# Two-block transformer on one core: modulations computed as dot products on VectorE, and tiles placed at multiples of 128 bytes

## The chip, the cores and the metric

One core of a Trainium2 chip runs the whole program. The metric is the device time of one execution in microseconds (us). About 0.5% is what a measurement of this kernel can tell from no change.

## What is computed

Batch 1, 512 latent tokens and 256 context tokens of 1024 channels, all in float32. The first block has two layers; each modulates its inputs by a condition vector `c` (latent) and `c_ctx` (context):

```python
for i in range(DEPTH):                      # 2 layers: windowed attention, then gated linear attention (GLA)
    m_lat = jnp.split((c_lat @ w_mod[i] + b_mod[i])[:, None, :], N_MOD, axis=-1)   # c_lat = silu(c)
    m_ctx = jnp.split(c_con @ w_mod[i] + b_mod[i], N_MOD, axis=-1)                 # c_con = silu(c_ctx)
    h_lat = modulate(x_lat, g_pre_mix[i], m_lat[0], m_lat[1])
    h_ctx = modulate(x_ctx, g_pre_mix[i], m_ctx[0], m_ctx[1])
    ...
def channel_mlp(h, w_in, w_out):
    return jnp.square(jax.nn.relu(h @ w_in)) @ w_out
```

`w_mod[i]` is 1024 x 6144, six modulations of 1024 numbers: m 0 and 1 shift and scale the mixer's input, 2 is the gate of its output, 3 to 5 the same for the MLP. A second block follows with a chunked attention, a state-space branch and a mixture of experts (MoE) of 16 experts, two per token.

## The kernel before, in words

Activations lie transposed in SBUF, channels on the partitions. A weight comes in units of 1 MB (128 x 2048 float32) by SP's queue into `raw`; `unit` (L209) splits it into two F32R tiles, `whi` by ScalarE (L213) and `wlo` by VectorE (L214), and every product is three F32R matmuls (`mm3`, `mm3s`, L229 to L244): high by high, high by low, low by high. In the first half of the MLP (`inproj`, L399) the weights are stationary and the activations `hl` (512 latent columns) and `hc` (256 context columns) move, in the second half (`natproj1`, L421, by `second`) the squared activations `hid` are stationary and 512 columns of the weights move. The MLP (L715) runs over 16 blocks of 256 hidden channels; in each it loads one unit of either matrix, does `first(b)` and `second([b - 1])`, squares on VectorE (L732, L733) and adds to `acc` on VectorE (L790). The order on each engine is the one in which the program is written, as a scheduler with priorities lays it out.

A modulation half (`mod_half`, L340) is 512 of the 1024 numbers of one m: two raw loads of 1 MB, 16 float32 matmuls with `csil` (silu of both condition vectors, padded to 32 columns) stationary and 256 weight columns moving (L354; 32 rows of the trace), a copy on ScalarE (L358), four transposes by `ident` on TensorE (L361), a sum and the bias on VectorE (L364, L366). 24 halves are computed: 4 in `first_norm`, 12 as filler between the score groups of `layer0_attn` (list `mods`, L562, L563), 8 between the heads of `layer1_mix` (L1076, L1115). The first MLP has no filler. `mod_affine` (L369) and `mod_gate` (L384) read what they give. In the GLA, `states` holds the recurrence over chunks (L1037, with S updated by VectorE at L1039), and L1055 to L1057 its outputs.

Constants are allocated first in one pool: `small` (vectors and biases), `ident`, `identb`, `mhalf`, then `csil`, `modT`, `aff`. Everything that comes after them, the pool of weight tiles first, begins where they end:

```python
self.c = e(tc.tile_pool(name="const", bufs=1))
self.w = e(tc.tile_pool(name="wstream", bufs=2))
```

Of the kernel before, what the change touches and what calls it, by code (L numbers as in the profile page):

```python
# [10 lines left out]
F32 = mybir.dt.float32  # L11
F32R = mybir.dt.float32r
BF = mybir.dt.bfloat16
I32 = mybir.dt.int32
U32 = mybir.dt.uint32
AF = mybir.ActivationFunctionType
ALU = mybir.AluOpType
AX = mybir.AxisListType
SP = mybir.EngineType.SP
P = 128  # L20
D = 1024
KC = 8
# [7 lines left out]
def _unit_in(w, c=256):  # L30
    k, n = w.shape
    return np.ascontiguousarray(
        w.reshape(k // P, P, n // c, c).transpose(2, 1, 0, 3).reshape(n // c, P, -1))


def _unit_out(w):
    k, n = w.shape
    return np.ascontiguousarray(
        w.reshape(k // 256, 2, P, n).transpose(0, 2, 1, 3).reshape(k // 256, P, -1))
# [37 lines left out]
def prep(i):  # L77
    o = {}
# [6 lines left out]
    cc[:, :, 1] = g("c_ctx").reshape(KC, P).T  # L85
    s.add("c", cc)
    for l in range(2):
        o[f"w_mod{l}"] = _unit_in(g("w_mod")[l])
        s.add(f"b_mod{l}", _cols(g("b_mod")[l]))
        for n in ("g_pre_mix", "g_post_mix", "g_pre_mlp", "g_post_mlp"):  # L90
            s.add(f"{n}{l}", _cols(g(n)[l]))
        o[f"w_mlp_in{l}"] = _unit_in(g("w_mlp_in")[l])
        o[f"w_mlp_out{l}"] = _unit_out(g("w_mlp_out")[l])
    o["w_qkv"] = _unit_in(g("attn_w_qkv")[0])
    perm = []
    for t in range(8):
# [51 lines left out]
class Kern:  # L148
    def __init__(self, tc, A, at):
        self.tc, self.nc, self.A, self.at = tc, tc.nc, A, at  # L150
        self.stack = ExitStack()
        e = self.stack.enter_context
        self.c = e(tc.tile_pool(name="const", bufs=1))
        self.w = e(tc.tile_pool(name="wstream", bufs=2))
        self.s = None
        self.t = e(tc.tile_pool(name="tiny", bufs=6))
        self.dram = e(tc.tile_pool(name="dram", bufs=1, space=bass.MemoryType.DRAM))
        self.p2 = e(tc.tile_pool(name="ps2", bufs=2, space=bass.MemoryType.PSUM))
        self.p1 = e(tc.tile_pool(name="ps1", bufs=4, space=bass.MemoryType.PSUM))
        nc = self.nc  # L160
        self.small = self.c.tile([P, A["small"].shape[1]], F32, name="small")
        nc.sync.dma_start(self.small, A["small"])
        self.ident = self.c.tile([P, P], F32, name="ident")
        make_identity(nc, self.ident)
        self.identb = self.c.tile([P, P], BF, name="identb")
        nc.vector.tensor_copy(self.identb, self.ident)
        self.n = 0
        self.norms = []
        self.sides = {"left": "left", "right": "right"}
        self.mhalf = self.c.tile([P, 4], F32, name="mhalf")  # L170
        nc.vector.memset(self.mhalf, -0.5)

    def right(self, name, bufs=1):
# [157 lines left out]

    def mod_init(self):
        nc = self.nc
        self.csil = self.c.tile([P, KC, 32], F32, name="csil")
        nc.vector.memset(self.csil, 0.0)
        nc.scalar.activation(self.csil[:, :, 0:2], self.sm("c").rearrange("p (k b) -> p k b", b=2), AF.Silu)
        self.modT = [self.c.tile([P, 48, 2], F32, name=f"modT{l}") for l in range(2)]
        self.aff = {}

    def mod_half(self, pool, l, m, half, tag="rows", raws=("raw", "raw"), own=None):  # L340
# [19 lines left out]
        for k in range(4):  # L360
# [5 lines left out]
        nc.vector.tensor_add(self.modT[l][:, c0:c0 + 4, :], self.modT[l][:, c0:c0 + 4, :],  # L366
                             bm[:, :, None].to_broadcast([P, 4, 2]))

    def mod_affine(self, l, which, ks=slice(0, KC)):  # L369

        nc = self.nc
        m0 = 0 if which == "mix" else 3
        if (l, which) not in self.aff:
            self.aff[l, which] = [self.c.tile([P, 2, KC], F32, name=self.nm("aff")) for _ in range(2)]
        sc, sh = self.aff[l, which]
        gp = self.sm(f"g_pre_{which}{l}")
        at = lambda m: slice(8 * m + ks.start, 8 * m + ks.stop)
        for b in range(2):
            nc.vector.scalar_tensor_tensor(sc[:, b, ks], self.modT[l][:, at(m0 + 1), b], 1.0, gp[:, ks],
                                           op0=ALU.add, op1=ALU.mult)  # L380
            nc.vector.tensor_copy(sh[:, b, ks], self.modT[l][:, at(m0), b])
        return sc, sh
# [96 lines left out]
def layer0_attn(K):  # L479
# [11 lines left out]
    with ExitStack() as left:  # L491
# [67 lines left out]
        op = K.opool.enter_context(K.right("oT"))  # L559
        oc = op.tile([P, KC, NCTX], F32, name="oTc")  # L560
        ol = op.tile([P, KC, L], F32, name="oTl")
        mods = [(0, m, x) for m in (2, 3, 4, 5) for x in range(2)]  # L562
        mods += [(1, m, x) for m in (1, 0) for x in range(2)]  # L563
        with K.right("att", 2) as ap:
            def scores(qb, j):

# [92 lines left out]
                pass  # L659
            w_o = [K.unit(A["w_o0"][u]) for u in range(2)]  # L660
            K.mod_affine(0, "mlp")
            K.mod_affine(1, "mix")
    return oc, ol, w_o


# [46 lines left out]
        finish(*last)  # L712


def mlp(K, l, hs, nts, finish, swap, side, split=False, filler=None):  # L715


    tc, nc, A = K.tc, K.nc, K.A
# [3 lines left out]
    with tc.tile_pool(name="mlp", bufs=1, side=side) as mp, tc.tile_pool(name="mlph", bufs=4, side=side) as hp:  # L722
# [74 lines left out]
        for b in range(1, NB):  # L797
            if b > 1:
                first(b)
            if b < NB - 1:  # L800
                second([b - 1])
            if filler and b == 1:

                z = hp.tile([P, nts[0] * P], F32, tag="hf0", name=K.nm("hf"), bufs=1)
                nc.vector.memset(z[:, 0:1], 0.0)
                K.anchor = z[:, 0:1]
            for _ in range(2 if filler else 0):
                next(filler, None)
        second([NB - 2, NB - 1])

# [1 line left out]
def layer0(K):  # L812
# [2 lines left out]
    oc, ol, w_o = layer0_attn(K)  # L815
    X = K.residual(K.ctx_pool)
    sc, sh = K.aff[0, "mlp"]
    sc1, sh1 = K.aff[1, "mix"]
    h = [None, None]
    hp, h_close = K.opened(K.left("h1l"))  # L820
    h[0] = K.pair(hp, "hl", [P, KC, L])
# [18 lines left out]
    with K.scratch(), K.right("gate") as gp:  # L840
        for i in (4, 5):
            pre(i, sc, sh, False)
        gates2 = []

        def swap():
            gates2.extend(K.mod_gate(0, "mlp", b, gp) for b in range(2))
            h_close.close()
            hp, K.h_close = K.opened(K.left("h2l"))
            hcp, K.hc_close = K.opened(K.left("h2c"))
            h[:] = [K.pair(hp, "hl", [P, KC, L]), K.pair(hcp, "hc", [P, KC, NCTX])]  # L850

        def finish2(i, y):
            K.postnorm(X[i], y, gates2[i // 4])
            pre(i, sc1, sh1, dv=2, pool=i < 4)
        mlp(K, 0, list(h), [4, 2], finish2, swap, "right")
    K.ctx_close.close()
    return X[:4], h

# [1 line left out]
def layer1_mix(K, hl, hc):  # L860
# [212 lines left out]
                nc.tensor.transpose(b[:, c * P:c * P + P], ys[c][:, t * P:t * P + P], K.ident)  # L1073
            a.copy(dst, b)

    mods = [(1, m, x) for m in (2, 4, 3, 5) for x in range(2)]  # L1076
    dec = {}
    tc.keep_in_program_order(a.preload_act_table_set("natural_log_exp_and_others"))
    u = K.unit(A["gla_in"][0])
# [24 lines left out]
    for h in range(6):  # L1104
        if h < 4:
            S[h] = states(h, dec[h])
        if h == 0:

            zero = K.tiny(1)
            v.tensor_scalar(zero, dec[3][1][2][:, 0, 0:1], 0.0, None, op0=ALU.mult)  # L1110
            for t in range(4):
                a.activation(og[:, t, :], og[:, t, :], AF.Silu, bias=zero)
                o = og[:, t, :].rearrange("p (h x) -> p h x", h=4)
                v.tensor_mul(o, o, gn[:, None, :].to_broadcast([P, 4, 256]))
        for i in range((2, 2, 1, 1, 1, 1)[h]):  # L1115
            K.mod_half(hp, *mods.pop(0), tag="ktc", raws=(("whi", "wlo"), ("raw", "raw"))[i])
        if 1 <= h < 5:
            Y[h - 1] = output(h - 1, *S[h - 1])
        if h >= 2:
            turn(*Y[h - 2])  # L1120
# [970 lines left out]
```

## Time and profile before

| what | us |
|---|---|
| median of 3 runs (2306.82 to 2314.99) | 2307.37 |
| the profiled execution | 2317.49 |
| its span | 2315.5 |
| TensorE busy (PE) | 2189.1 |
| VectorE busy (DVE) | 1307.3 |
| ScalarE busy (ACT) | 968.4 |
| GpSimd busy (POOL) | 284.2 |

Engine names in rows: PE is TensorE's matmuls, PEld its weight loads beside them, DVE VectorE, ACT ScalarE, POOL GpSimd, SP the engine that issues most DMAs. PEclk is the granted clock of TensorE, 1.00 its full 2.4 GHz. Matmuls overlap in the pipeline: one lasts longer in a row than the next one's start is behind its own, so that the distance of two starts tells what one costs. L12 is line 12 of the kernel. "a<-b" is a result and what it is computed from, with the number of the tile left out; of a matmul the operand that moves stands first.

### The profile page before, as it was taken

The page shows a single profiled execution, that of the slowest core. Times are in us where ns is not written, and L with a number is a line of the kernel's source. Part 1 is how long each engine was busy: PE and PEld are TensorE (multiplying, and loading weights), DVE is VectorE, ACT ScalarE, POOL GpSimd, SP SyncE. Part 2 cuts the span into 40 slices and gives each one's busy share as a digit, 9 for nine tenths or more (in the row PEclk, how much of TensorE's full clock was granted, in tenths as well). Part 3 has the DMA queues.
Part 4 walks back from the last instruction along what each step waited for, and adds up shares of the span by engine and source line. Part 5 has one row for each costly group of instructions (what it writes and reads, how often), then busy time and mean ns, then how long its engine had stood idle before and what let it go on. Part 6 is the DMA issues. An engine that isn't in the chain of part 4 may idle for free. (4 is left out here: it accounts for less than half of the span.)

```text
span 2315.5 us, 31205 instructions
## 1 busy us (share of the span) xinstructions
PE 2189.1 (95%) x12608; PEld 1795.7 (78%) x12608; DVE 1307.3 (56%) x2203; ACT 968.4 (42%) x1515; POOL 284.2 (12%) x301
## 2 busy tenths in 40 slices
PE   7999989999999999899999999999989997897996
PEld 5876658888888888789967887888789875686775
DVE  4666664435454444631864578555645854447885
ACT  5445555521121222542544543232354453435874
POOL 0024432000000000500000100000130000012321
PEclk9999999999999999999999999999999998998998
DMA  7223341211221121202353133422332335568993
GB/s 285 73 92 128 128 168 51 73 55 55 73 73 55 55 73 55 71 37 70 115 197 130 51 109 112 143 96 91 111 104 91 135 128 112 140 247 292 314 306 106
DMA packets 53746, 278.10 MB, mean 120 GB/s; under 512 B 8864, under 2 KB 13360, under 8 KB 25184
## 3 DMA queue, kind: packets, MB, share of 16 engines
q1 hardware_dynamic: 42080, 248.75, 30.7%
q0 software_dynamic: 10704, 25.68, 3.8%
q8 instruction: 100, 1.64, 0.3%
q10 hardware_dynamic: 816, 1.66, 0.2%
q14 instruction: 46, 0.38, 0.0%
HBM read 263.49 MB, written 24.08 MB: 124 GB/s over the span
## 5 line engine op out<-in xcount | busy, mean ns | idle before, releaser
L213 ACT CAST whi<-raw 128x2048 fp32r<-128x2048 f32 x106 | 202.4, 1910 | 551.2 <-PE b L244 381.6
L214 DVE TENSOR_TENSOR wlo<-raw,whi 128x2048 fp32r<-128x2048 f32 x106 | 245.2, 2315 | 270.8 <-ACT whi L213 264.9
L242 PE MATMUL b<-hl,whi 128*128 128x512 f32 (+1 forms) x736 | 284.0, 386 | 2.4 <-DVE t L315 1.8
L790 DVE TENSOR_TENSOR acc<-acc,b 128x512 f32<-128x512 f32 x280 | 179.9, 681 | 187.5 <-PE b L244 187.3
L240 PE MATMUL b<-hl,whi 128*128 128x512 f32 (+1 forms) x736 | 282.9, 385 | 0.8 <-ACT whi L213 0.8
L244 PE MATMUL b<-hl,wlo 128*128 128x512 f32 (+1 forms) x736 | 281.8, 386 | 0.0
L242 PE MATMUL b<-wlo,hid 128*128 128x512 f32 x640 | 216.1, 394 | 0.0
L240 PE MATMUL b<-whi,hid 128*128 128x512 f32 x640 | 214.8, 395 | 0.7 <-DVE acc L790 0.7
L244 PE MATMUL b<-whi,hid 128*128 128x512 f32 x640 | 214.0, 395 | 0.0
L242 PEld LDWEIGHTS b<-hl,whi 128*128 128x128 f32 x736 | 139.2, 189 | 30.3 <-issue 2.9
L240 PEld LDWEIGHTS b<-hl,whi 128*128 128x128 f32 x736 | 138.9, 189 | 30.2 <-ACT whi L213 1.3
L244 PEld LDWEIGHTS b<-hl,wlo 128*128 128x128 f32 x736 | 139.3, 189 | 28.2 <-issue 0.2
L1947 DVE TENSOR_TENSOR wlo<-raw,whi 128x2048 fp32r<-128x2048 f32 x57 | 129.8, 2286 | 32.0 <-ACT whi L1947 32.0
L242 PEld LDWEIGHTS b<-wlo,hid 128*128 128x128 f32 x640 | 120.4, 188 | 27.7
L244 PEld LDWEIGHTS b<-whi,hid 128*128 128x128 f32 x640 | 120.2, 188 | 27.8
L240 PEld LDWEIGHTS b<-whi,hid 128*128 128x128 f32 x640 | 119.4, 189 | 27.3 <-DVE acc L790 1.2
L604 POOL TENSOR_TENSOR p<-p,t 128x512 f32<-128x512 f32 (+2 forms) x96 | 91.7, 970 | 186.0 <-DVE modT L364 90.3
L1947 ACT CAST whi<-raw 128x2048 fp32r<-128x2048 f32 x57 | 108.3, 1912 | 10.3 <-PE b L234 10.3
L232 PE MATMUL b<-whi,hl 128*128 128x256 f32 x320 | 91.2, 285 | 2.3 <-ACT qr L1455 2.3
L233 PE MATMUL b<-wlo,hl 128*128 128x256 f32 x320 | 91.5, 286 | 0.0
L234 PE MATMUL b<-whi,hl 128*128 128x256 f32 x320 | 91.2, 285 | 0.0
L601 ACT ACTIVATE p<-b,t 128x513 f32<-128x513 f32 (+2 forms) x96 | 62.4, 654 | 49.9 <-DVE t L593 49.5
(609 smaller groups left out, 4711.1 us busy)
## 6 DMA issues: line engine op xcount, KB each, us to landing
raw<-in_w_e_dram SPq DMA_DIRECT2D x57, 1024.0 KB, 7.0
raw<-in_w_mod_dram SPq DMA_DIRECT2D x48, 1024.0 KB, 7.6
raw<-in_w_mlp_in_dram SPq DMA_DIRECT2D x32, 1024.0 KB, 4.8
raw<-in_w_mlp_out_dram SPq DMA_DIRECT2D x32, 1024.0 KB, 4.9
raw<-in_w_in_dram SPq DMA_DIRECT2D x16, 1024.0 KB, 5.3
raw<-in_gla_in_dram SPq DMA_DIRECT2D x12, 1024.0 KB, 4.7
raw<-in_w_o_dram SPq DMA_DIRECT2D x8, 1024.0 KB, 5.2
raw<-in_w_qkv_dram SPq DMA_DIRECT2D x6, 1024.0 KB, 17.5
```

Source lines behind the costliest of these rows:

```text
L213: ins = self.nc.scalar.copy(hi, r).ins
L214: ins = ins, (self.nc.gpsimd if pool else self.nc.vector).tensor_sub(lo, r, hi.bitcast(F32)).ins
L232: mm(out, ah, bh, start=start, stop=False)
L233: mm(out, ah, bl, start=False, stop=False)
L234: mm(out, al, bh, start=False, stop=stop)
L240: mm(o, ah, b, start=start, stop=False)
L242: mm(o, ah, b, start=False, stop=False)
L244: mm(o, al, b, start=False, stop=stop)
L601: nc.scalar.activation(p[:, :n], S[:, a0:a0 + n], AF.Exp, bias=nmx[:, g:g + 1], accum_out=den[:, g:g + 1])
L604: nc.gpsimd.tensor_mul(p[:, :n - 1], p[:, :n - 1], den[:, g:g + 1].to_broadcast([P, n - 1]))
L790: nc.vector.tensor_add(a, a, bs[n])
L1947: ins = K.nc.scalar.copy(hi, r).ins, K.nc.vector.tensor_sub(lo, r, hi.bitcast(F32)).ins
```

## The change

Two things are done. **Modulations.** 14 of the 24 halves go: the last six of attention's list and the eight of the GLA. Their numbers (m 5 of layer 0, all of layer 1) are computed by `mod_dots`, as a filler of the first MLP, four steps per block. A step loads one tile `mw` of 128 outputs x 1024 inputs (float32, 512 KB, 56 of them, three buffers) by GpSimd's DMA queue and multiplies it on VectorE with the broadcast silu of a condition vector (`cb`), summing along the row: `tensor_tensor_reduce`, 32 of them for m 0 and 1 of layer 1 and 16 for m 5 of layer 0 (both vectors), 32 for m 2 to 5 of layer 1 (latent alone), 80 in all; each is two rows on VectorE, the product and the read of the accumulator. The two `cb` are loaded on ScalarE's queue. `mod_affine(1, "mix")` is called inside; `finish2` reads its result later. The product itself, written to a bfloat16 tile, is not used.

**Places.** `ident`, `identb` and `csil` are allocated ahead of `small`, and `mhalf` and one `aff` go to a pool at the other end of SBUF. In the two programs the tiles' first bytes (in a partition) are:

| tile | before | past a multiple of 128 | after | past |
|---|---|---|---|---|
| ident | 18240 | 64 | 16512 | 0 |
| csil | 19040 | 96 | 17280 | 0 |
| whi | 37984, 46176 | 96 | 37888, 46080 | 0 |
| wlo | 54368, 62560 | 96 | 54272, 62464 | 0 |
| hl (first MLP's input) | 88288, 104672 | 96 | 88192, 104576 | 0 |
| third whi, wlo of the MoE | 184384, 192576 | 64 | 184288, 192480 | 96 |

Counted over the programs by the place of the two operands, F32R matmuls of 256 columns: 3,472 with both 96 past before, the same 3,472 at 0 after; of 512 columns: 5,208 both 96 past, then at 0; 432 with the moving operand 96 past and the stationary one 64 past, then 0 and 96; 312 with both 64 past, then 96. The float32 matmuls are 2,078 before and 1,798 after.

```diff
@@ prep
-        o[f"w_mod{l}"] = _unit_in(g("w_mod")[l])
+    o["w_mod0"] = _unit_in(g("w_mod")[0][:, :5 * D])
+    turned = lambda w: np.ascontiguousarray(w.T).reshape(-1, P, D)
+    o["w_modT"] = np.concatenate([turned(g("w_mod")[0][:, 5 * D:]), turned(g("w_mod")[1])])
+    o["cc"] = np.stack([g("c")[0], g("c_ctx")])
@@ Kern.__init__
+        self.ident = self.c.tile([P, P], F32, name="ident")
+        self.identb = self.c.tile([P, P], BF, name="identb")
+        self.csil = self.c.tile([P, KC, 32], F32, name="csil")
         self.small = self.c.tile([P, A["small"].shape[1]], F32, name="small")
         nc.sync.dma_start(self.small, A["small"])
-        self.ident = self.c.tile([P, P], F32, name="ident")
         make_identity(nc, self.ident)
-        self.identb = self.c.tile([P, P], BF, name="identb")
...
-        self.mhalf = self.c.tile([P, 4], F32, name="mhalf")
+        edge = e(tc.tile_pool(name="edge", bufs=1, side="right"))
+        self.mhalf = edge.tile([P, 8], F32, name="mhalf")
+        self.edge_aff = edge.tile([P, 2, KC], F32, name="edge_aff")
@@ mod_init
-        self.csil = self.c.tile([P, KC, 32], F32, name="csil")
...
+        nc.vector.memset(self.modT[1], 0.0)
@@ new
+    def mod_dots(self, gp, wp):
+        nc, v = self.nc, self.nc.vector
+        cb = [gp.tile([P, D], F32, tag=f"gate{b}", name=self.nm("cb")) for b in range(2)]
+        for b in range(2):
+            nc.scalar.dma_start(cb[b], self.A["cc"][b:b + 1, :].to_broadcast([P, D]))
+            nc.scalar.activation(cb[b], cb[b], AF.Silu)
+        n = 0
+        for l, m in [(0, 5)] + [(1, m) for m in range(6)]:
+            bs = range(2 if l == 0 or m < 2 else 1)
+            to = self.modT[l][:, 8 * m:8 * m + 8]
+            for k in range(8):
+                w = wp.tile([P, D], F32, tag="mw", name=self.nm("mw"), bufs=3)
+                nc.gpsimd.dma_start(w, self.A["w_modT"][n])
+                n += 1
+                for b in bs:
+                    junk = self.s.tile([P, D], BF, tag="junk", name=self.nm("junk"))
+                    v.tensor_tensor_reduce(junk, w, cb[b], 1.0, 0.0, ALU.mult, ALU.add, to[:, k, b:b + 1])
+                if k == 7:
+                    to = to[:, :, 0:len(bs)]
+                    v.tensor_add(to, to, self.sm(f"b_mod{l}")[:, 8 * m:8 * m + 8, None].to_broadcast([P, 8, len(bs)]))
+                    if (l, m) == (1, 1):
+                        self.mod_affine(1, "mix")
+                yield
@@ layer0_attn
-        mods = [(0, m, x) for m in (2, 3, 4, 5) for x in range(2)]
-        mods += [(1, m, x) for m in (1, 0) for x in range(2)]
+        mods = [(0, m, x) for m in (2, 3, 4) for x in range(2)]
...
-            K.mod_affine(1, "mix")
@@ mlp
-            for _ in range(2 if filler else 0):
+            for _ in range(steps):
                 next(filler, None)
@@ layer0
-            pre(i, sc1, sh1, dv=2, pool=i < 4)
-        mlp(K, 0, list(h), [4, 2], finish2, swap, "right")
+            pre(i, *K.aff[1, "mix"], dv=2, pool=i < 4)
+        mw, mw_close = K.opened(K.left("mw"))
+        mlp(K, 0, list(h), [4, 2], finish2, swap, "right", filler=K.mod_dots(gp, mw), steps=4)
@@ layer1_mix
-    mods = [(1, m, x) for m in (2, 4, 3, 5) for x in range(2)]
...
-        for i in range((2, 2, 1, 1, 1, 1)[h]):
-            K.mod_half(hp, *mods.pop(0), tag="ktc", raws=(("whi", "wlo"), ("raw", "raw"))[i])
```

VectorE in the first MLP, in the order of issue, before: the sums of the second half (`acc`) and the squares (`hf`, `hid`).

```order
L790 TENSOR_TENSOR acc_4115<-acc_4115,b_4627 128x512
L790 TENSOR_TENSOR acc_4115<-acc_4115,b_4628 128x512
L732 TENSOR_TENSOR hf_4611<-hf_4611 128x512
L732 TENSOR_TENSOR hf_4616<-hf_4616 128x256
L790 TENSOR_TENSOR acc_4116<-acc_4116,b_4643 128x512
L790 TENSOR_TENSOR acc_4116<-acc_4116,b_4644 128x512
L733 TENSOR_TENSOR hid_766_4608<-hf_4611,hid_765_4607 128x512
L733 TENSOR_TENSOR hid_768_4610<-hf_4616,hid_767_4609 128x256
L790 TENSOR_TENSOR acc_4117<-acc_4117,b_4659 128x512
L790 TENSOR_TENSOR acc_4117<-acc_4117,b_4660 128x512
L790 TENSOR_TENSOR acc_4118<-acc_4118,b_4675 128x512
L790 TENSOR_TENSOR acc_4118<-acc_4118,b_4676 128x512
```

After, at one such place (L823 is the sum that was L790; L395 are the dot products, one row for the product and one for the accumulator):

```order
L823 TENSOR_TENSOR acc_3939<-acc_3939,b_5043 128x512
L395 ISA junk_6885,modT_100<-mw_6883,cb_4310 128x1024
L395 ISA modT_100 128x1
L823 TENSOR_TENSOR acc_3939<-acc_3939,b_5044 128x512
L395 ISA junk_6889,modT_100<-mw_6887,cb_4310 128x1024
L395 ISA modT_100 128x1
L395 ISA junk_7127,modT_100<-mw_7125,cb_4310 128x1024
L395 ISA modT_100 128x1
L823 TENSOR_TENSOR acc_3940<-acc_3940,b_5059 128x512
L823 TENSOR_TENSOR acc_3940<-acc_3940,b_5060 128x512
L395 ISA junk_7131,modT_100<-mw_7129,cb_4310 128x1024
L395 ISA modT_100 128x1
```

The dot products stand in VectorE's queue between the sums, from row 409 to row 684 of that queue: from just before the first MLP, between the norms of `hc`, to its fifth block, 13 or 14 in a block.

TensorE in the GLA before, between the recurrence (L1037) and the outputs (L1055 to L1057), with two modulation halves (L354, L361):

```order
L1037 MATMUL b_9904<-zv,ktl_9874 128x256
L1037 MATMUL b_9911<-zv,ktl_9874 128x256
L1037 MATMUL b_9918<-zv,ktl_9874 128x256
L354 MATMUL b_9937<-raw_9938,csil 32x256 x8
L354 MATMUL b_9937<-raw_9948,csil 32x256 x8
L1055 MATMUL b_1494_10123<-zv,AT_9884 128x256
L1056 MATMUL b_1494_10123<-S_9902,qd_9175 128x256
L1037 MATMUL b_9904<-zv,ktl_9882 128x256
L361 MATMUL b_9960<-ident,rows_9958 128x128 x4
L1037 MATMUL b_9911<-zv,ktl_9882 128x256
```

After, the same place (L1071 was L1037, L1089 and L1090 were L1055 and L1056, L1030 is the next head's transposes, which was L996):

```order
L1071 MATMUL b_10017<-zv,ktl_9987 128x256
L1071 MATMUL b_10024<-zv,ktl_9987 128x256
L1071 MATMUL b_10031<-zv,ktl_9987 128x256
L1030 MATMUL b_10050<-ident,ki_9397 128x128 x2
L1030 MATMUL b_10050<-ident,zk 128x128 x2
L1089 MATMUL b_1581_10116<-zv,AT_9997 128x256
L1090 MATMUL b_1581_10116<-S_10015,qd_9288 128x256
L1071 MATMUL b_10017<-zv,ktl_9995 128x256
```

The next head's transposes and the outputs now stand directly behind the recurrence's steps.

GpSimd's queue after, at the end of the norms ahead of the first MLP, with the first tiles of the dot products:

```order
L266 TENSOR_TENSOR t_3738<-t_3737,mhalf 128x1
L266 TENSOR_TENSOR t_3822<-t_3821,mhalf 128x1
L391 DMA mw_4316<-in_w_modT_dram 128x1024
L391 DMA mw_4322<-in_w_modT_dram 128x1024
L391 DMA mw_4328<-in_w_modT_dram 128x1024
L266 TENSOR_TENSOR t_3840<-t_3839,mhalf 128x1
L266 TENSOR_TENSOR t_3869<-t_3868,mhalf 128x1
L266 TENSOR_TENSOR t_3900<-t_3899,mhalf 128x1
L391 DMA mw_4334<-in_w_modT_dram 128x1024
```

The first three loads stand ahead of the last small powers of the norms; the next ones follow, each behind a buffer that comes free.

## Rows read from the trace of the kernel before

**Rows 1.** The page's busy times (us, share of span) and granted clock in 40 slices.

```profile
PE 2189.1 (95%) x12608; PEld 1795.7 (78%) x12608; DVE 1307.3 (56%) x2203; ACT 968.4 (42%) x1515; POOL 284.2 (12%) x301
...
PEclk9999999999999999999999999999999998998998
```

**Rows 2.** Windows, a middle block of the first MLP (us, busy, count, PEclk, DMA share, GB/s).

```profile
522.51:556.08 33.57, 33.57 (x170) 28.31 (x169) 15.95 (x23) 7.11 (x10) 0.00 (x0) 1.00 0.18 63
```

**Rows 3.** Timeline of TensorE in a block of the first MLP (start, duration in us).

```profile
708.01 0.39 PE L240 MATMUL b<-hl,whi 128*128 128x512 f32 x1
708.24 0.28 PE L240 MATMUL b<-hc,whi 128*128 128x256 f32 x1
708.36 0.39 PE L242 MATMUL b<-hl,whi 128*128 128x512 f32 x1
708.59 0.28 PE L242 MATMUL b<-hc,whi 128*128 128x256 f32 x1
...
709.06 0.40 PE L240 MATMUL b<-hl,whi 128*128 128x512 f32 x1
```

**Rows 4.** Timeline of TensorE in the MoE, weights 64 past, then 96 past.

```profile
2143.86 0.39 PE L233 MATMUL b<-wlo,x 128*128 128x512 f32 x1
...
2144.56 0.39 PE L233 MATMUL b<-wlo,x 128*128 128x512 f32 x1
...
2148.49 0.40 PE L232 MATMUL b<-whi,x 128*128 128x512 f32 x1
...
2148.95 0.39 PE L234 MATMUL b<-whi,x 128*128 128x512 f32 x1
...
2149.65 1.03 PE L1935 MATMUL b<-ident,x 128*128 128x128 f32 x8
```

**Rows 5.** Groups of TensorE in the GLA, 1165 to 1255 (busy us, mean ns).

```profile
L354 PE MATMUL b<-raw,csil 128*32 128x256 f32 x256 | 18.7, 383 | 0.0
...
L361 PE MATMUL b<-ident,rows 128*128 128x128 f32 x32 | 5.0, 278 | 1.1 <-ACT rows L358 0.9
```

**Rows 6.** Windows of the GLA and of the MoE.

```profile
1165.00:1255.00 90.00, 82.84 (x608) 61.43 (x607) 51.99 (x109) 38.39 (x81) 4.07 (x4) 0.97 0.48 177
2110.00:2300.00 190.00, 179.66 (x870) 142.37 (x868) 154.06 (x110) 143.18 (x128) 50.64 (x31) 0.98 0.80 268
```

**Rows 7.** Windows of six groups of four heads in attention, L354 alone.

```profile
234.60:246.30 11.70, 1.93 (x32) 0.94 (x32) 1.00 0.06 10
246.30:252.80 6.50, 0.00 (x0) 0.00 (x0) 1.00 0.75 311
252.80:260.50 7.70, 1.93 (x32) 0.94 (x32) 1.00 0.12 18
260.50:267.60 7.10, 0.00 (x0) 0.00 (x0) 1.00 0.67 278
267.60:276.80 9.20, 1.93 (x32) 0.94 (x32) 1.00 0.04 10
276.80:282.80 6.00, 0.00 (x0) 0.00 (x0) 1.00 0.87 295
```

**Rows 8.** Groups of VectorE in the second attention (busy us, mean ns).

```profile
L1535 DVE CUSTOM_DVE_ANT_0 s<-b,tb 128x512 f32<-128x512 f32 x8 | 5.5, 689 | 11.4 <-PE b L1533 7.4 <-ACT whi L213 4.0
...
L1535 DVE DVE_READ_ACCUMULATOR2_ANT t<- 128x1 f32 x32 | 2.7, 83 | 0.0
...
L1535 DVE CUSTOM_DVE_ANT_0 s<-b,tb 128x128 f32<-128x128 f32 x8 | 2.3, 289 | 4.8 <-issue 4.3 <-PE b L1533 0.5
```

**Rows 9.** Windows of the stretch that the dot products fall into.

```profile
410.00:474.00 64.00, 63.47 (x338) 54.01 (x337) 24.58 (x33) 34.07 (x62) 2.03 (x3) 1.00 0.19 66
474.00:597.00 123.00, 123.00 (x621) 103.96 (x620) 58.66 (x80) 26.99 (x40) 0.00 (x0) 1.00 0.20 69
```

**Rows 10.** DMA issues of GpSimd's queue (count, KB each, us to landing).

```profile
w<-ssm_w POOLq DMA_DIRECT2D x4, 512.0 KB, 4.7
...
x<-h_rows,tab POOLq DMA_INDIRECT x19, 9.7
```

More of the change, by code (lines that the diff above doesn't have):

```diff
@@ L373, in mod_affine @@
         if (l, which) not in self.aff:
-            self.aff[l, which] = [self.c.tile([P, 2, KC], F32, name=self.nm("aff")) for _ in range(2)]
+            tiles = [self.c.tile([P, 2, KC], F32, name=self.nm("aff")) for _ in range(1 if not self.aff else 2)]
+            self.aff[l, which] = tiles + ([self.edge_aff] if not self.aff else [])
         sc, sh = self.aff[l, which]
@@ L712, in out_full, with mlp @@
         finish(*last)
-def mlp(K, l, hs, nts, finish, swap, side, split=False, filler=None):
+def mlp(K, l, hs, nts, finish, swap, side, split=False, filler=None, steps=2):
     tc, nc, A = K.tc, K.nc, K.A
@@ L801, in mlp @@
                 second([b - 1])
-            if filler and b == 1:
+            if l and b == 1:
                 z = hp.tile([P, nts[0] * P], F32, tag="hf0", name=K.nm("hf"), bufs=1)
@@ L817, in layer0 @@
     sc, sh = K.aff[0, "mlp"]
-    sc1, sh1 = K.aff[1, "mix"]
     h = [None, None]
@@ L845, in swap @@
         def swap():
+            mw_close.close()
             gates2.extend(K.mod_gate(0, "mlp", b, gp) for b in range(2))
```

## The prediction

> **What bounds the kernel now.** I read the page's busy times first, then the windows of one stretch after another, then single matmuls. TensorE is busy 95% of the span, at a granted clock of nine tenths or more in every slice [rows 1]; no other engine comes near it. So what counts is how many matmuls there are, how long each takes, and the few stretches where TensorE waits. The profiled execution took 2317.49 us, 10.1 us (0.4%) above the median of 2307.37; the sum is made against 2317.5 and brought down by 0.4% at the end. About 0.5% (11.5 us) is what a measurement of this kernel can tell from no change.
>
> A middle block of the first MLP shows the steady state: 33.57 us long, TensorE busy in all of it, VectorE in 15.95 us, ScalarE in 7.11 us, DMA share 0.18 [rows 2]. Nothing waits there, yet it is not at the clock's pace. A block has 120 matmuls of 512 columns and 48 of 256 (counted from `inproj` and `second`), that is 73,728 columns, which at 2.4 GHz, the level of the granted 1.00, are 30.72 us. The other 2.85 us are 17 ns per matmul. The timeline shows where: starts at 708.01, 708.24, 708.36, 708.59 and, after three pairs, 709.06 [rows 3], so 1.05 us for three pairs; a 512 follows after 0.231 us (213.3 by its columns) and a 256 after 0.12 us (106.7). The excess is 17.7 ns in a long one and 13.3 ns in a short one: nearly a constant per matmul, not a share of its columns.
>
> **The change part by part.**
>
> *Alignment.* Tiles that began 96 bytes past a multiple of 128 now begin on one. In the two programs 3,472 F32R matmuls of 256 columns and 5,640 of 512 (of 9,532) move their moving operand from 96 past to 0, 9,112 in all. No row of before has an F32R moving operand at 0, so the price is bounded. Upper end: 13.3 ns, the whole excess of a 256, which is the time of 32 columns of 4 bytes, as if one more piece of 128 bytes had to be fetched where a row straddles 9 of them and not 8. By that reading a 512 loses 13.3 of its 17.7. Lower end: nothing, or a loss of a few ns, for two rows speak against it: in the MoE the matmuls whose weights begin 64 past (from 2143.55) start at 2143.86 and, three on, at 2144.56, 0.233 apart, and those 96 past at 2148.49 and, two on, 2148.95, the same 0.23 [rows 4]. 64 past straddles one piece more as well, so they agree with the upper end too; they exclude only that 64 would be enough. The eight 128-column transposes of L1935 take 1.03 us less one's duration of 0.28 (as at L361), over 7 = 107 ns each [rows 4, 5], which is two passes of 53.3: nothing over, though their moving `ident` begins 64 past. So there is no constant cost of 13 ns per instruction; either two passes leave a piece too many the time to hide, or the excess belongs to F32R by itself and the start does not matter. Between the ends I take 11 ns, near the upper one, because the 256's 13.3 and the length of one piece agree so closely: 9,112 x 11 = 100 us. Less what is not on the path: MoE, where DMA is at 0.80 and TensorE idles in 10 of 190 us [rows 6]; scores in attention that wait for others; and five MLP blocks in which VectorE becomes full (below); together 16 us. **−84 us**, ends 0 and −105.
>
> The Trainium skill ("SBUF — State Buffer", section Specifications (TRN2)) gives cachelines of 16 bytes, with a penalty for each cross to a new line. By it a tile 96 or 64 past already begins on a line, the number of lines read is the same, and this term would be 0: that is the first rival below; the equal pitches of rows 4 agree with it, and no run so far shows a start at 0.
>
> *Attention: six modulation halves go* (layer 0's m 5, layer 1's m 1 and 0, from the second half of the heads loop). Six neighbouring groups of four heads, with one half and without by turns, last 11.7, 6.5, 7.7, 7.1, 9.2 and 6.0 us [rows 7]: sums 28.6 and 19.6, 3.0 us per half. TensorE's own work in one is 1.93 us of matmuls [rows 7] and four transposes of 107 ns, 2.4 us. 6 x 2.4 = 14, 6 x 3.0 = 18. I take the lower, **−14 us**: exp and bias on ScalarE, VectorE and GpSimd stay, and TensorE will wait for them more.
>
> *GLA: eight halves go.* In the 90 us from 1165 to 1255 L354 is busy 18.7 us and L361 5.0 [rows 5], and TensorE idles 7.2 us [rows 6]. All of it gone would be −24. But the state recurrence (L1037 to L1039) remains, each step waiting for VectorE's S; the halves were filler between its steps. Lower end −5, if most gaps open. I take a little over half, **−13 us**. The raw loads behind them leave SP's queue (28 MB), which brings the next units' weights earlier; nobody waits for those on TensorE here, so 0.
>
> *First MLP: dot products.* 80 `tensor_tensor_reduce` of 1024 elements. The same kind of instruction at L1535 takes 689 ns for 512 and 289 for 128, 1.04 ns per element, and an accumulator read 83 ns [rows 8]: 1222 + 83 = 1.305 us, times 80 = **104 us on VectorE**. They run from just before the first MLP to its fifth block. In those 187 us VectorE is busy 24.58 + 58.66 = 83.2 us now [rows 9]; with 104.4 that is 187.6 of 187. VectorE becomes full there. Behind a dot in its queue stand wlo (L214), the squares (L732, L733) and acc (L790), for which TensorE waits. With two weight sets and six banks as slack it should nearly keep pace: **+8 us**, ends 0 and +25 (a quarter of the dots' time on the path).
>
> *Tiles for the dots.* 56 loads of 512 KB on GpSimd's queue, three buffers, while SP brings 1 MB per unit at a share of 0.20 [rows 9]. 187 us / 56 = one per 3.3 us. The same size on that queue lands after 4.7 us, the slowest kind after 9.7 [rows 10]. With three buffers and 1.3 to 2.6 us of dots per tile plus about 1 us of hand-over, a tile comes each (4.7 + 1.9 + 1)/3 = 2.5 us: in time, 0. On GpSimd the first three issues stand ahead of the last small powers of hc's norms; the later ones wait there for buffers, with nothing else behind them, since GpSimd is busy 0.00 us from 474 to 597 [rows 9]: 0. Two Silu and two loads on ScalarE's queue ahead of the MLP, whose ScalarE is half idle: 0 (at most +3). The late `mod_affine(1, "mix")` is done by the third block, its reader is in the last: 0. Moved `mhalf` and the memset: 0.
>
> **Sum:** −14 −13 +8 −84 = −103; 2317.5 − 103 = 2214.5; times 2307.4/2317.5 gives **2205 us**.
>
> **The rivals.** (A) *The excess is not the start of the tile.* Pitches stay at 0.231 and 0.12; only −19 remain: 2298.5, **2288 us** (2277 to 2300). For it: 64 and 96 past are alike, and transposes with a start 64 past show no excess [rows 4]. Against: nothing else in the rows explains a nearly constant 13 to 18 ns.
> (B) *A, and VectorE takes back what the halves gave:* −27 + 25 = −2, **2305 us**. For it: 187.6 of 187 [rows 9]. Against: it needs the upper end of that bound with nothing hidden.
> (C) *Slower: the tiles arrive late.* VectorE takes its instructions in order; a dot whose tile has not landed holds wlo and acc behind it, and TensorE then stands. At a landing of 9.7 us [rows 10] a tile comes each (9.7 + 1.9 + 1)/3 = 4.2 us, 0.9 late, of which 0.1 may hide in slack: 56 x 0.8 = +45. Without the alignment's gain −27 + 45 = +18, **2325 us**. It decides from a landing of about 7.5 us. For it: GpSimd's queue carries no load in this stretch now, and VectorE is full. Against: 4.7 us for the same size [rows 10], at a DMA share of 0.20. With the alignment's gain it would give 2241, inside the range.
> The Trainium skill ("SBUF — State Buffer", "The 'DVE blocks DMA' trap (SWDGE)") has a way for C to come about: GpSimd cannot write descriptors while VectorE runs some of its faster modes. No row of before has such a load beside a busy VectorE.
>
> **How the numbers follow.** Both parts work, 0.57: 2205, own range 2162 (−105 by alignment, dots −42) to 2242 (8 ns, dots −5). A 0.23, B 0.12, C 0.08. The range runs from 2165 to 2300 and leaves out B and C (0.20). Faster than 2296: the first case and most of A, 0.57 + 0.20 = 0.77; slower than 2319: C, 0.08; the rest, 0.15, within 0.5%.
>
> **What would show it.** Alignment right: an MLP block that the dots don't reach (9 to 14) falls from 33.57 to about 33.57 − 168 x 0.011 = 31.7 us, short pitches to 0.107 to 0.11 us, long ones to 0.22; at 33.5 it is A. Attention: groups in the second half all near 6.5 us. GLA: its window of 90 us about 13 us shorter, with more idle ahead of L1037 and L1055. Dots: 80 rows near 1.22 us; VectorE over 95% from hc's norms to the fifth block and TensorE waiting there under 10 us; waits of VectorE on loads of mw near 0, and landings below 7 us. If the first MLP's early blocks take over 36 us with VectorE idle on mw, it is C; with VectorE busy, B.

## The result, and the profile after

The changed kernel takes 2286.02 us (median of 4 runs, 2284.00 to 2290.45); before, measured beside it, takes 2309.18. The ratio is 0.9899, with a 95% interval of 0.9873 to 0.9924: 1.0% or some 23 us faster, where 102 us were forecast. That is the first rival's time (2288 us: the dot products pay, the new places of the tiles do nothing). The profiled execution took 2287.39 us, its span 2285.7 us; the spans of the two profiles differ by 29.8 us, more than the medians, since before's profiled execution (2317.49) lay 8 us over its median.

The page's busy times and DMA queue of GpSimd after (beside [rows 1]; the queue's columns are packets, MB, share of the DMA engines):

```profile
PE 2147.8 (94%) x12104; PEld 1773.3 (78%) x12104; DVE 1391.3 (61%) x2343; ACT 963.6 (42%) x1504; POOL 321.6 (14%) x357
...
q0 software_dynamic: 18768, 55.04, 7.6%
```

TensorE still bounds the kernel: it has 504 matmul rows and 41 us less to do, VectorE 84 us more. Now the same pairs of a first-MLP block as in [rows 3], from the timeline of TensorE after:

```profile
704.19 0.39 PE L248 MATMUL b<-hl,whi 128*128 128x512 f32 x1
704.42 0.28 PE L248 MATMUL b<-hc,whi 128*128 128x256 f32 x1
704.54 0.39 PE L250 MATMUL b<-hl,whi 128*128 128x512 f32 x1
704.76 0.28 PE L250 MATMUL b<-hc,whi 128*128 128x256 f32 x1
...
705.24 0.40 PE L248 MATMUL b<-hl,whi 128*128 128x512 f32 x1
```

1.05 us for three pairs, to the hundredth what it was, though every tile in it now begins at a multiple of 128 bytes. To see where the time went, the same matmul is looked up in both timelines. Before:

```profile
390.32 0.62 PE L242 MATMUL b<-wr,oh 128*128 128x512 f32 x2
...
724.12 0.64 PE L240 MATMUL b<-whi,hid 128*128 128x512 f32 x2
...
940.07 0.39 PE L244 MATMUL b<-whi,hid 128*128 128x512 f32 x1
...
1295.27 0.62 PE L242 MATMUL b<-wr,oh 128*128 128x512 f32 x2
...
2302.76 0.63 PE L244 MATMUL b<-whi,g 128*128 128x512 f32 x2
```

After:

```profile
382.08 0.62 PE L250 MATMUL b<-wr,oh 128*128 128x512 f32 x2
...
720.30 0.64 PE L248 MATMUL b<-whi,hid 128*128 128x512 f32 x2
...
936.25 0.39 PE L252 MATMUL b<-whi,hid 128*128 128x512 f32 x1
...
1267.24 0.62 PE L250 MATMUL b<-wr,oh 128*128 128x512 f32 x2
...
2268.44 0.63 PE L252 MATMUL b<-whi,g 128*128 128x512 f32 x2
```

The lead is 8.2 us behind attention, 3.8 in the middle of the first MLP (the dots cost 4.4), and still exactly 3.8 some 216 us and six blocks later: 215.95 us in either program, over a thousand matmuls, with the places of their tiles changed. Then it is 28.0 us behind the GLA (a gain of 24), 34.3 at the last matmul, and 29.8 at the end of the span: the last stretch takes 4.5 us longer. Of the 6.3 us between the GLA and the last matmul 5.6 are waits in the state-space branch (15.0 us in this profile of before, 9.4 in this one of after), which are taken up below.

### The profile page after: what moved, and what is told of

Read it like the earlier page. It is cut to its first block, busy times and chain, and to the rows that moved or that the text cites. A ratio compares the mean times of both kernels' runs of the same rounds, so it can differ in the third digit from the quotient of the medians.

```text
span 2285.7 us, 30405 instructions
## 1 busy us (share of the span) xinstructions
PE 2147.8 (94%) x12104; PEld 1773.3 (78%) x12104; DVE 1391.3 (61%) x2343; ACT 963.6 (42%) x1504; POOL 321.6 (14%) x357
## 3 DMA queue, kind: packets, MB, share of 16 engines
q0 software_dynamic: 18768, 55.04, 7.6%
## 5 line engine op out<-in xcount | busy, mean ns | idle before, releaser
L823 DVE TENSOR_TENSOR acc<-acc,b 128x512 f32<-128x512 f32 x280 | 180.8, 682 | 157.0 <-PE b L252 156.7
L395 DVE CUSTOM_DVE_ANT_0 junk<-mw,cb 128x1024 bf16<-128x1024 f32 x80 | 97.5, 1219 | 3.2 <-DMA mw<-in_w_modT_dram 2.6
```

What stands on the lines that cost most here:

```text
L395: v.tensor_tensor_reduce(junk, w, cb[b], 1.0, 0.0, ALU.mult, ALU.add, to[:, k, b:b + 1])
L823: nc.vector.tensor_add(a, a, bs[n])
```

## The experiments

**The two parts apart.** e1_places is the kernel before with the new places of `ident`, `identb`, `csil`, `mhalf` and one `aff` alone. e2_dots_96 is the kernel after with 96 bytes ahead of the constants, so that weights and activations begin 96 bytes past a multiple of 128 again; `hid` of both MLPs stays at 0:

```diff
+        self.pad = self.c.tile([P, 24], F32, name="pad")
         self.ident = self.c.tile([P, P], F32, name="ident")
```

> The kernel before with the new places alone: all 24 halves stay on TensorE, tiles begin at multiples of 128 bytes. Theory 1 (the start of a tile is worth nothing): ratio to before 0.998 to 1.002, a middle block of the first MLP 33.57 us as before, starts of 512-column matmuls 0.231 us apart. Theory 2 (the start is worth 11 ns per matmul and the dot products ate it): ratio about 0.964, a middle block about 31.7 us.

2304.88 us (10 runs) beside 2310.64: ratio 0.9972, 0.9947 to 0.9998. In its profile the matmuls that before start at 940.07 and 1650.24 come 0.66 and 2.6 us earlier, and the first-MLP stretch from 430 to 940 is the same within 0.05 us. So a start at 0 is worth 0 in this stretch. The ratio is just under the 0.998 that was expected and its interval ends just under 1; where these 6 us come from is open, but they are a fourteenth of the 84 forecast.

> The kernel after with 96 bytes put ahead of the constants, so that weights and activations begin 96 bytes past a multiple of 128 again (hid of the first MLP stays at 0); the dot products stay. Theory 1: as the kernel after, ratio to before 0.988 to 0.992, stretch from 609 us on as in after within 0.3 us. Theory 2: slower than after by some 3%, ratio about 1.02.

2288.92 us, ratio 0.9904, 0.9871 to 0.9937: the kernel after. Dots and removed halves make the gain with the old starts as with the new ones. The second theory falls.

**What a matmul costs by itself.** e3_pitch and e6_grid are new kernels of chains such as

```python
for i in range(32):
    nc.tensor.matmul(b, w[:, o + 128 * (i % 2):o + 128 * (i % 2) + 128], m[:, 512 * (i % 4) + p:512 * (i % 4) + p + 512], ...)
```

with other starts o of the stationary and p of the moving operand.

> Chains of 32 matmuls alone on a chip, on zeros, the rest of the computation left out, after 128 to warm the clock: 512 columns of F32R from starts 0, 96, 64 and 4 bytes past a multiple of 128, stationary operand 96 past too, one stationary operand for all, one moving slice for all, 256 and 128 columns at 0 and 96, bfloat16 at 0 and 96, and pairs of 512 and 256 as in the kernel. Theory 1: all F32R chains of 512 stand at 0.231 us whatever the start, 256 at 0.12, and bfloat16 tells whether the excess of 17 ns belongs to F32R (bfloat16 then near 0.216) or to every matmul. Theory 2: 0.218 to 0.22 at 0, 0.231 at 96. A third: the excess comes from exchanging the stationary operand, then one operand for all gives less than 0.22.

The timeline of e3 (a row is a chain; the start of the next less its own, over 32, is the pitch, good to some 0.3 ns with starts rounded to 10 ns): L40 both starts at 0, L43 the moving one 96 bytes on, L52 both 96 bytes on, L73 and L76 bfloat16.

```profile
36.90 7.42 PE L40 MATMUL b<-m,wr 128*128 128x512 f32 x32
44.16 7.64 PE L43 MATMUL b<-m,wr 128*128 128x512 f32 x32
51.63 7.51 PE L46 MATMUL b<-m,wr 128*128 128x512 f32 x32
...
66.58 7.42 PE L52 MATMUL b<-m,wr 128*128 128x512 f32 x32
73.84 7.46 PE L55 MATMUL b<-m,wr 128*128 128x512 f32 x32
...
103.16 7.08 PE L73 MATMUL b<-mb,wb 128*128 128x512 bf16 x31
110.08 7.07 PE L76 MATMUL b<-mb,wb 128*128 128x512 bf16 x31
116.98 3.66 PE L79 MATMUL b<-mb,wb 128*128 128x256 bf16 x32
```

226.9 ns, 233.4 with one operand moved by 96 bytes, and 226.9 again with both moved. With the moving start 64 bytes on a matmul takes 229.5, with 4 bytes on 237.6. One stationary operand for all gives 227.9 and one moving slice for all 226.7, so the third theory falls: exchanging the stationary operand is not the excess. 256 columns take 119.7 at 0 and 120.0 at 96; 128 columns 110 and 112, which is 57 over their 53.3, so the excess is not the same for every matmul either. bfloat16 takes 216.3 and 215.6. So most of the excess belongs to F32R and stayed at every start tried, and some 6 ns of a long one hang on how the two starts lie to each other. None of the three theories had said that; it is the theory of the next run.

The Trainium skill ("TensorE: Matmul & The Clock Gate", "Wait — 56ns, not 53.3ns?") gives 215.7 ns for 512 columns back to back. The bfloat16 chains agree; the F32R ones stand 11 ns above it.

> Again chains of 32 F32R matmuls of 512 columns on zeros, the rest of the computation left out: the four starts 0, 32, 64 and 96 of the stationary operand against the same four of the moving one, then the stationary operand moved on by 128 bytes to 16 KB, the kernel's strides, two banks by turns, and chains beside a busy VectorE and a busy ScalarE. Theory 1 (only the distance of the two starts modulo 128 bytes counts, which the change leaves at 0 where it was 0): the four cells with equal starts stand at 0.227 us, cells with 96 between them at 0.233, whatever the moving start itself is. Rival (the moving start alone counts): rows with equal moving start agree, and 96 against 96 stands at 0.233; the pair of equal starts of the first such run was then chance. Neighbours on VectorE and ScalarE change nothing by either.

Rows of its timeline: L40 both at 0, L43 the moving operand 96 on, L55 both 96 on, L60 to L62 the stationary one 128, 256 and 512 bytes on; behind each but the last the chain whose start ends it.

```profile
53.34 7.42 PE L40 MATMUL b<-m,w 128*128 128x512 f32 x32
60.60 7.63 PE L41 MATMUL b<-m,w 128*128 128x512 f32 x32
...
75.40 7.64 PE L43 MATMUL b<-m,w 128*128 128x512 f32 x32
82.88 7.62 PE L44 MATMUL b<-m,w 128*128 128x512 f32 x32
...
164.46 7.43 PE L55 MATMUL b<-m,w 128*128 128x512 f32 x32
171.73 7.57 PE L56 MATMUL b<-m,w 128*128 128x512 f32 x32
...
201.26 7.61 PE L60 MATMUL b<-m,w 128*128 128x512 f32 x32
208.71 7.46 PE L61 MATMUL b<-m,w 128*128 128x512 f32 x32
216.01 7.42 PE L62 MATMUL b<-m,w 128*128 128x512 f32 x32
223.26 7.42 PE L63 MATMUL b<-m,w 128*128 128x512 f32 x32
```

All the pitches of the first sixteen chains, in ns:

| stationary starts at | moving at 0 | 32 | 64 | 96 |
|---|---|---|---|---|
| 0 | 226.9 | 233.4 | 229.1 | 233.7 |
| 32 | 233.1 | 226.9 | 233.4 | 229.4 |
| 64 | 232.8 | 233.1 | 226.9 | 233.4 |
| 96 | 234.1 | 233.1 | 233.1 | 227.2 |

The diagonal is what is fast: the distance counts, not the start. But it does not repeat at 128 bytes, as the expectation had it: 128 apart cost 232.8, 256 cost 228.1, and 512 and every doubling up to 16 KB 226.6 to 226.9. Chains beside a busy VectorE or ScalarE stood at 226.7. Pairs of 512 and 256 columns, as in the first half of the MLP but with all operands at a distance of 0, are the chain L72, 24 pairs:

```profile
284.92 8.63 PE L72 MATMUL b<-m,w 128*128 128x512 f32 x48
293.39 10.82 PE L74 MATMUL b<-m,w 128*128 128x512 f32 x47
```

A pair takes 353 ns, 236.0 for the long one and 116.9 for the short one, where the two alone take 226.7 and 119.7, 346 together; the pairs of e3 show the same. In pairs a distance of 0 is no gain.

With that the real kernels were read again. In before, 3,894 of some 5,960 F32R matmuls of 512 columns have the stationary operand 384 bytes past the moving one (modulo 512), most of them hl by whi and whi by hid in both MLPs; in after it is the same 3,894. That distance was in no chain. In the trace of before those stand at 232.0 ns on average, 432 at a distance of 480 at 233.4, those at 0 at 229.6 (median 228), counted where the records of both neighbours are there. Where a long one follows a long one, 384 stands at 232.6, 128 at 232.4, 256 at 228.1 and 0 at 228.9 (median 227), near what the chains give for 128, 256 and 0. The change had moved all tiles together. The pad of e2 did not: by it 2,166 matmuls, whi by hid above all, went from 384 to 288, and stayed slow (in the second MLP 232.8 ns against 232.4 in after).

**The distances set to 0.** In e10_before_gaps and e8_gaps (and e9) a gap goes ahead of hl in three pools (h1l, h2l, h3) and ahead of the MLP's own tiles:

```diff
     hp, h_close = K.opened(K.left("h1l"))
+    K.nc.vector.memset(hp.tile([P, 96], F32, name="gap"), 0.0)
...
+        nc.vector.memset(mp.tile([P, 96], F32, name=K.nm("gap")), 0.0)
         acc = [mp.tile([P, D], F32, name=K.nm("acc")) for _ in range(ntile)]
```

> The kernel before with a gap of 384 bytes ahead of hl (of both layers and the GLA) and of the MLPs' right-hand tiles, nothing else: tiles still begin 96 bytes past a multiple of 128 (weights) but 3,552 F32R matmuls of 512 columns go from a distance of 384 to a distance of 0 (modulo 512) between the starts of the two operands. Theory 1 (the distance modulo 512 counts, not the start): 232.0 down to 227 to 229 ns for each of them, 10 to 18 us in all, ratio to before 0.992 to 0.996, and a middle block of the first MLP, with 120 such matmuls, 33.57 down to 33.0 to 33.2 us. Rival (the start modulo 128 counts): no change, 33.57 us.

2295.43 us beside 2312.09, ratio 0.9933, 0.9911 to 0.9954, with starts 96 bytes past a multiple of 128 as before. Two matmuls in its timeline, the first at 940.07 in before:

```profile
933.30 0.39 PE L244 MATMUL b<-whi,hid 128*128 128x512 f32 x1
...
1634.21 0.39 PE L240 MATMUL b<-hl,whi 128*128 128x512 f32 x1
```

The second in before:

```profile
1650.24 0.40 PE L240 MATMUL b<-hl,whi 128*128 128x512 f32 x1
```

They are 6.8 and 16.0 us earlier: 2.9 of it from 430 to 940 in the first MLP and 8.3 from 1293 to 1650 in the second, which has only matmuls of 512 columns. There every group of them, hl and whi by hid alike, fell from between 232.4 and 232.6 ns to between 226.6 and 227.0, as the chains have it. In the first MLP a block gained 0.2 us and not 0.4 to 0.6: whi by hid fell from 232.9 to 229.0 ns, but in the pairs of 512 and 256 the long one rose from 229.0 to 235.3 while the short one fell from 120.6 to 117.2, so there nothing is won: these are the 236.0 and 116.9 of the chain of pairs.

> The kernel after with the same gaps. Theory 1: 10 to 18 us below the kernel after, ratio to before 0.982 to 0.986, middle blocks of the first MLP past the dots 33.0 to 33.2 us. Rival: as after, 0.989 to 0.990.

2278.48 us, ratio 0.9852, 0.9830 to 0.9873: by the ratios about 10 us under after, the lower edge of what was expected.

**What the dots cost.** e4_no_dots has `filler=iter(())`, sets `modT` to zero and calls `mod_affine(1, "mix")` ahead of the MLP.

> The kernel after without the dot products and their loads: layer 1's modulations and the last of layer 0 are left out (zeros in their place). What the dots cost in the first MLP is the difference to after. If the 4.5 us that the first MLP lost against before are theirs: 0.2% below after, ratio to before 0.986 to 0.990, and the first MLP 4 to 5 us shorter. If they cost nothing and the loss is the clock's own course after attention: the same time as after and the first MLP as long.

Its total (2273.32 us, ratio 0.9818) can't be used, since with other modulations the second block gets other data, and the MoE, whose work depends on them, ran 6 us shorter. The first MLP can be used: from 390 us to 940 after loses 4.5 us against it, as against before (4.4). Where, is seen in windows of after (us, then busy time of PE, PEld, DVE, ACT, POOL with counts, PEclk, DMA share, GB/s), and in its waits of TensorE from 400 to 620; the last line is the only wait of before there:

```profile
440.00:450.00 10.00, 9.50 (x46) 8.59 (x47) 9.07 (x16) 3.85 (x9) 1.05 (x2) 0.83 0.61 213
450.00:597.00 147.00, 147.00 (x748) 124.44 (x747) 135.41 (x222) 37.09 (x56) 23.22 (x44) 1.00 0.66 225
```

```profile
PE b L248 <- ACT whi L221: 1.9, 1, 1.9
PE b L250 <- DVE t L323: 1.5, 1, 1.5
```

```profile
PE b L242 <- DVE hl L302: 0.5, 1, 0.5
```

From 450 to 597 VectorE is busy 135 of 147 us and TensorE all 147 at full clock: the full VectorE costs nothing in this stretch. The loss is one wait of 1.9 us for whi, which ends at 440.5, with the clock granted at 0.83 of full speed in the 10 us behind it (1.7 us), and 1.0 us more at the wait for hc's norm. The wait for whi comes from the order on TensorE: in after 48 matmuls of hc stand between the last one of hl and the first that needs the new whi, in before and in e4 72. ScalarE's cast to whi (1.90 us) begins in either when the last reader of its buffer is done; in before TensorE has the other 24 matmuls of hc to do meanwhile, in after they come behind and it waits for the whole cast. The wait is there in the five profiles with 48 (both of after, e2, e8, e12) and in none of the other seven of full kernels, which have 72.

> The kernel after with each dot product held, by the order of VectorE's queue, behind the latest sum or square of the block in which it was written, so that the 80 spread over 14 blocks of the first MLP at 5 to 6 a block. If the early crowding on VectorE is what the dots cost: the first MLP 3 to 5 us shorter than in after, ratio to before 0.986 to 0.989, about 0.2% below the kernel after of this call. If it is the dots' number: no shorter, the same time as after.

```diff
+                        K.pace = nc.vector.tensor_add(a, a, bs[n]).ins
...
+                    i = v.tensor_tensor_reduce(junk, w, cb[b], 1.0, 0.0, ALU.mult, ALU.add, to[:, k, b:b + 1]).ins
+                    self.tc.add_manual_dep(i, self.pace.name, mybir.DependencyInfo(
+                        mybir.DependencyClass.NoSync, mybir.DependencyReason.DATA), reason="paced")
```

> The kernel after as it is, on the chip of this call, as the measure for the paced one: ratio to before 0.988 to 0.992; and a second profile of it, by which the waits on loads of the state-space branch that differ between the profiles so far can be seen again: 9 to 11 us of TensorE's waits there if the place of the tiles sets them, anything from 9 to 15 if they vary by themselves.

2281.78 us paced and 2285.41 as it is, ratios 0.9886 (0.9861 to 0.9911) and 0.9896 (0.9874 to 0.9918): the intervals overlap, so the times don't show a gain. In the profile TensorE's order has 72 matmuls of hc ahead of that whi again, the wait for it is gone and the stretch from 430 to 940 is 3.6 us shorter than in after. The wait for hc's norm stays at 1.5 us, so the dots' place on VectorE does not make it; what does is open. The second profile of after also shows how much two executions of one program differ: attention took 3.7 us less than in the first, with the granted clock at 1.00 in it and not 0.97. The waits in the state-space branch, which looked as if they followed the places (15 us with 96, 9 to 11 with 0), were 13.9 us in it, at 0; they vary by themselves, and nothing is concluded from them.

> The paced dot products and the gaps together, as the candidate that beats both kernels. If the two effects add: about 3 us below the run with gaps alone, ratio to before 0.980 to 0.985; if pacing is worth nothing, the same as that run.

2271.39 us, ratio 0.9826, 0.9805 to 0.9848. It beats both kernels: 1.7% under before and outside after's interval.

**The end.** The 4.5 us behind the last matmul recur in each kernel that loads the tiles on GpSimd's queue. The last DRAIN there, from the rows of the program's closing line (count: shortest/median/longest ns, first and last start), before and after:

```profile
L2087 POOLq DRAIN  x3: 46/113/2437, 2312.3 to 2315.3; - x3
```

```profile
L2118 POOLq DRAIN  x3: 46/109/6193, 2278.7 to 2285.4; - x3
```

Before its queue carried 10,704 packets and after 18,768. e12_after_sp and e11_sp_queue (on top of e9) change one line:

```diff
-                nc.gpsimd.dma_start(w, self.A["w_modT"][n])
+                nc.sync.dma_start(w, self.A["w_modT"][n])
```

> The kernel after with one line changed: the tiles of the dot products are loaded on SP's queue and not on GpSimd's. Theory (the last DRAIN and semaphore update of GpSimd grow with what went through its queue: 2.44 and 0.77 us at 10,704 packets, 6.19 and 1.69 at 18,768): back to 2.44 and 0.77 us, 4.7 us off the end, ratio to before 0.987 to 0.989. Rival: the end stays, and since loads of weights now stand behind loads that wait for a dot product on SP's queue, TensorE waits for weights in the first MLP: the first MLP longer than in after by several us, ratio 0.990 to 0.995.

```profile
L2118 POOLq DRAIN  x3: 46/112/2437, 2268.2 to 2271.2; - x3
```

2.44 us again, and the first MLP as long as in after within 0.1 us: SP's queue held nothing back. In the profile the span ends 12.7 us behind the end of TensorE's last matmul, against 16.6 in after. The total, 2287.06 us (2273.50 to 2294.25), ratio 0.9906, 0.9887 to 0.9925, does not show the 4.7 us; in six runs they drown in the spread. That the drain shrinks is shown, that the kernel does is not.

> Paced dot products, gaps and the loads on SP's queue. If the three effects add: 4 to 5 us below the paced kernel with gaps, ratio to before 0.978 to 0.982, the last DRAIN of GpSimd 2.44 us. If SP's queue holds weights back: above that kernel, with TensorE's waits on whi or wlo in the first MLP.

2269.55 us, ratio 0.9817, 0.9797 to 0.9837: the fastest of all, 1.8% under before, but 1.8 us under e9 is not clear of the noise.

## Why the prediction was wrong, point by point

- **The step that failed: "Between the ends I take 11 ns, near the upper one, because the 256's 13.3 and the length of one piece agree so closely".** The excess was put down to where the moving tile begins, because a short matmul's 13.3 ns is as long as 32 columns. That was chance: 256 columns take 119.7 ns with the start at 0 and 120.0 with it at 96. Measured, a start at 0 is worth 0 (215.95 us against 215.95 in the first MLP; e1; the diagonal of the grid). What counts, some 6 ns of a long one, is the distance of the two operands, with the multiples of 512 bytes fast, and the change left every distance alone: the table of places shows both operands move by the same 96 bytes, and [rows 4] compared a distance of 0 with one of 480, whose 229.6 and 233.4 ns a reading in steps of 10 ns over two or three matmuls can't tell apart. The other 11 to 13 ns are F32R's own; why F32R has them no run shows. So −84 became 0, the lower end of that term, and rival A's time came.
- **The transposes.** That there is "no constant cost of 13 ns per instruction" was drawn from two-pass instructions [rows 4, 5] and did not hold for F32R, where 256 columns cost 13 ns over their columns at any start.
- **Attention, −14.** 8.2 us in this pair of profiles. From 230 us to the same matmul TensorE is busy 12.2 us less but waits 3.9 us more:

```profile
230.00:338.30 108.30, 104.18 (x827) 67.27 (x824) 68.08 (x158) 56.61 (x137) 48.29 (x52) 0.98 0.41 153
```

```profile
230.00:330.00 100.00, 92.01 (x610) 60.11 (x608) 63.88 (x139) 54.03 (x131) 48.22 (x52) 0.97 0.10 38
```

  The first row is before, the second after. The second profile of after would make the gain 12.4 us, but it had the clock at 1.00 in attention and before 0.98. At 1.00 in both, the kernel before with gaps (e10) and that second profile take to the matmul that is at 390.32 in before:

```profile
229.64:386.69 157.04, 151.08 (x1046) 105.08 (x1045) 92.42 (x191) 82.42 (x183) 56.62 (x60) 1.00 0.36 132
```

```profile
229.57:377.92 148.34, 138.06 (x830) 96.80 (x829) 88.08 (x172) 79.93 (x177) 56.59 (x60) 1.00 0.15 55
```

  That is 8.7 us less: 13.0 us less work and 4.3 us more waiting. The work was sized right (14), and the reason given for taking the lower bound (the other engines' steps stay, and TensorE will wait for them) was right too; the waiting was put too low.
- **GLA, −13.** 23.7 us (a lead of 28.0 behind it, of 4.3 at 1150 us), the upper bound of 24: nearly all of the removed work was on the path. The recurrence's own waits, which were to open, come to 0.2 us; the waits of 4.2 us (L1089) and 2.5 us (L1107) that did open stand against 2.8, 2.5 and 2.1 us of others before.
- **First MLP, +8.** 4.4 us, but not by the mechanism given: from 450 to 597 VectorE was 92% busy without harm. One early wait for whi with its clock, 3.6 us, comes from TensorE's order, which is another where the dots are crowded; the other 1.0 us is at hc's norm. The price per dot (1.305 us) was right: 1.219 and 0.081.

```profile
L395 DVE CUSTOM_DVE_ANT_0 junk<-mw,cb 128x1024 bf16<-128x1024 f32 x80 | 97.5, 1219 | 3.2 <-DMA mw<-in_w_modT_dram 2.6
L395 DVE DVE_READ_ACCUMULATOR2_ANT modT<- 128x1 f32 x80 | 6.5, 81 | 0.0
```

- **The tiles, 0.** They landed after 4.5 us (page of after), as the row of the same size had it [rows 10], beside a VectorE that was 92% busy, and VectorE waited 2.6 us for them in all: rival C did not come, nor B. What nobody priced is the 4.7 us at the end of GpSimd's queue.
- **The sum** without alignment was −19 and measured −23 on the medians; the terms as measured, −8.7 −23.7 +4.4 +4.7, give the same. That rival A's 2288 us came within 2 us of the time is in part luck: attention gave 5 us less than its term, the GLA 11 more, the first MLP cost 4 less, and the end's 4.7 were in no term. The mechanism of the halves was right, in the GLA within its bounds and in attention below them; the large term was not there.

## What to carry to other kernels

If a change moves both operands of an instruction alike, ask what depends on their difference before pricing the move of one; a count of "now at 0" says nothing. Measure a disputed constant by a chain of the bare instruction first: one run of 129 us showed that the start alone is worth nothing, which the whole trace had left open. Leave two operands of an F32R matmul of 512 columns a multiple of 512 bytes apart when gaps are free (8.3 us in the second MLP), but not in pairs of 512 and 256 columns, where nothing was won. Compare attention with attention only at the same granted clock: 0.98 against 1.00 made 8.7 us look like 12.4.

## What the runs showed of the hardware that was not expected

- F32R, 512 columns at full clock: 226.6 to 227.2 ns at distances of 0 modulo 512 bytes, 228.1 at 256, 229 to 229.5 with the moving operand 64 later and 233 with it 64 earlier, 231 to 234 at 16, 32, 48, 80, 96 and 128, 237.6 at 4, but 226.8 at 112. No rule is offered for that list. The Trainium skill ("SBUF — State Buffer", Specifications (TRN2)) has a penalty by 16-byte cachelines; the diagonal of the grid, equal within 0.3 ns at four starts that are multiples of 16, agrees with it, and the cost beside the diagonal hangs on how two operands lie to each other.
- F32R in pairs of 512 and 256 columns that share the stationary operand: 236.0 and 116.9 ns at a distance of 0, 7 ns a pair more than the two alone.
- The closing drain of GpSimd's queue: 2.437 us (and a semaphore update of 0.772) at 10,704 packets, 6.193 (and 1.686) at 18,768, the same to the nanosecond in all twelve profiles of full kernels.
